# Output projection by token instance: 24 products per bank, and a last pass by token quarters

## The chip, the cores and the metric

The kernel runs on one core of a Trainium2 chip. The metric is device time in microseconds (us), the median of several executions. The core has five engines that run side by side and wait for each other through semaphores: TensorE (PE, with its weight loads shown as PEld), VectorE (DVE), ScalarE (ACT), GpSimd (POOL) and SyncE (SP). In this kernel nearly all transfers are issued by SP, in the order of its queue (SPq in the rows).

## The reference, cut to what matters

One decoder layer for a prompt of 1024 tokens and 8 sample tokens, 1032 tokens in all, with 1024 model columns. Everything is float32. The part that matters here:

```python
h = rmsnorm(x, w['norm1_w'])
proj = h @ w['w_in']
...                                   # HGRN2 heads -> o_a (1024 columns), Mamba-2 SSD -> y (1024 columns)
x = x + jnp.concatenate([o_a, y], axis=-1) @ w['w_out']
h = rmsnorm(x, w['norm2_w'])
gate, val = jnp.split(h @ w['w_up'], 2, axis=-1)
gate, buf_f_new = causal_dwconv(gate, buf_f, w['ffn_conv_w'], w['ffn_conv_b'])
x = x + (jax.nn.silu(gate) * val) @ w['w_down']
```

## The kernel before, in words

All activations lie transposed: 128 columns of the model per tile, tokens along the free axis. The 1032 tokens are four quarters of 258 (`QW`). Two quarters are an *instance* of the up projection (`hf` or `i` is 0 or 1). A float32 product is made of three matmuls on rounded halves (`steps`, `split`, `split_in`): weight high x activation high, high x low, low x high. So each weight block and each activation row is *split*: ACT casts the high half (`wh`, `mh`, `uh`), DVE subtracts to get the low half (`wl`, `ml`, `ul`). In this text a *product* is one such 128x128 by 258-column matmul on PE.

The order on PE is the order in which the code issues it (`manual_schedule`). Each PE step of the projections is one `tick`; `after(n, work)` issues work n ticks later, and `spread(pieces, n)` issues one piece every n ticks. The order on the other engines is made by the framework's planner from the dependences and the order of issue. `jobs` is the list of weight blocks in turn. When a job begins, the next one's weights are loaded (`load_ahead`, `wload`): one 512 KB DMA into `ws` (two buffers), the cast into `wh` and the subtraction into `wl` (two buffers each). `drive` mixes the steps of a stream, such as a `head`, between the products of the jobs up to a named one. `fetch` queues a load on SP behind the latest weight load.

The output projection has 16 row tiles: 0 to 7 from the HGRN heads, 8 to 15 from the SSD mixer. Each row tile lies in DRAM (`mix_d`); a head's tile is written at the end of that head (L1007). The jobs before:

- `o8.m` and `o12.m`: four row tiles, 256 output columns, all four token quarters, 96 products a job, a bank of 12 products each. The first sums are copied by ACT (L1076), the others added by DVE (L1078). The residual input is transposed on PE and added (`residual`). Head 7 runs beside the first of these jobs, up to `o12.2`.
- then for each instance `o0.m` and `o4.m`: four row tiles, 256 output columns, two quarters, 48 products a job. After the last four row tiles `final` stores the sum to `x1_d`, squares it on ACT and adds the square to `rst` on POOL.

So there are 24 weight blocks of 512 KB and 1536 products, and 128 banks are read out, 96 of them by DVE.

`set_norm` turns `rst` of one quarter into the second norm's factor. `set_of(i)` makes the seven operands p1 to p7 of the up projection from instance i (a seven-product scheme over two halves of the columns and two quarters of the tokens): `norm` scales the sums in place (L1171), `comb` makes sums and differences (L1189), `put` splits an operand (L1181, L1182). Before, `set_of` holds four temporaries of tag x5, which has five buffers, and the first up-projection weights (`up_load(0)`, two tiles of tag x5) are loaded inside `set_of(0)`, between `put` calls. POOL adds the weight sums (L1246) and `up_split` splits them (L1265, L1266). `set_of(0)` is issued beside the second instance's `o0` and `o4` jobs, `set_of(1)` 33 ticks into the first up step, whose products go first through instance 0, then through instance 1 (`ups(0, ...)`, 84 products each).

Of the kernel before, what the change touches and what calls it, by code (L numbers as in the profile page):

```python
# [1 line left out]

# [14 lines left out]
P = 128  # L17
DM = 1024
T = 1024
ND = 8  # L20
# [4 lines left out]
H = 8  # L25
# [25 lines left out]
def hybrid_layer(  # L51
# [219 lines left out]
    def drive(stream, weight, name):  # L271

        last = next(i for i, j in enumerate(jobs) if j[0] == name)
        left = sum(j[1] is not None for j in jobs[at[0]:last + 1]) * MMS
# [508 lines left out]
    def residual_load(m):  # L783
        ms = slice(m * P, (m + 1) * P)
        xs = [tl("d", "xs")[:, :512] for _ in range(2)]
        xd = small.tile([ND, P], F32, tag="xd", name=nm("xd"))
        for i in range(2):
            fetch(xs[i].rearrange("p (i m) -> p i m", m=P),
                  x_prompt[0, i * 512:(i + 1) * 512, ms].rearrange("(i p) m -> p i m", p=P))
        fetch(xd, x_sample[:, 0, ms])  # L790
        return xs, xd

    def residual(out, xs, xd):

        def add(x_, ps):
            V.tensor_tensor(x_, x_, ps, op=ALU.add)

        for i0 in range(2):
            ps = bank("xtp")
            for i in range(4):  # L800
                PE.transpose(ps[:, blk[i]], xs[i0][:, blk[i]], ident)
            if i0 == 0:
                add(out[0][:, 0:512], ps)
                ps = bank("xtd", "nx")
                PE.transpose(ps[:, :ND], xd, ident[:ND, :ND])
                add(out[1][:, 508:516], ps[:, :ND])
            else:
                add(out[0][:, 512:516], ps[:, 0:4])
                add(out[1][:, 0:508], ps[:, 4:512])
            yield  # L810
# [209 lines left out]
    def mix_load(r0):  # L1020

        lo = [tl("hT", "ml", F32R) for _ in range(4)]
        hi = [tl("hT", "mh", F32R) for _ in range(4)]
        for cs in chunks:
            for k in range(4):
                fetch(lo[k][:, cs].bitcast(F32), mix_d[r0 + k, :, cs])
        mixes[r0] = hi, lo

        def splits():
            for cs in chunks:  # L1030
                for k in range(4):
                    split_in(hi[k], lo[k], cs)
                    yield

        unsplit[r0] = splits()

    def split_rest(r0):
        for _ in unsplit[r0]:
            pass
# [455 lines left out]
```

## Time and profile before

| what | value |
|---|---|
| runs, us | 1795.12, 1800.53, 1799.58; median 1799.58 |
| the profiled execution's span, us | 1794.6 |
| PE busy | 1741.0 us, 97% |
| DVE busy | 1116.6 us, 62% |
| ACT busy | 789.1 us, 44% |
| POOL busy | 409.8 us, 23% |
| granted PE clock, mean | 0.992 |
| moved by DMA | 182.34 MB, mean 102 GB/s |

The span runs from the first to the last instruction of one profiled execution; the times of the runs hold what lies around it too. A busy time is the sum of the instructions' durations. Matmuls are pipelined and overlap in the record, so PE's speed is read from how far apart products start, or from how many of them a window holds. The output projection's products run from about 840 to 1065 us of the span, the first up step follows.

### The profile page before, as it was taken

How to read it: one execution, taken by the hardware profiler on the slowest of the kernel's cores; microseconds unless marked ns; L12 is line 12 of the kernel's file. 1: busy time of each engine (PE TensorE's matmuls, PEld its weight loads, DVE VectorE, ACT ScalarE, POOL GpSimd, SP SyncE). 2: the span in 40 equal slices, each digit the busy share in tenths (PEclk: the TensorE clock that was granted, in tenths of full speed). 3: DMA queues.
4: the chain of work that ended last, by engine and by line, in shares of the span. 5: the costliest groups of instructions: out<-in, count | busy, mean ns of one | idle time of the engine just before them, and what ended most of it. 6: DMA issues, size and time to landing. Idle time of an engine off the chain costs nothing.

```text
span 1794.6 us, 38584 instructions
## 1 busy us (share of the span) xinstructions
PE 1741.0 (97%) x16215; PEld 1685.0 (94%) x16215; DVE 1116.6 (62%) x2002; ACT 789.1 (44%) x1414; POOL 409.8 (23%) x415
## 2 busy tenths in 40 slices
PE   7999899999999999999999988999999999999998
PEld 7998798999999999999999978999999999999997
DVE  4658967556555564557746769666666667555545
ACT  6477688454544444345323344333433334111114
POOL 1103331110110110110100364455444542000001
PEclk9999999999999999999999998999999999999999
DMA  5135634553222221235334431222222225422212
GB/s 154 36 98 155 171 100 138 175 147 99 72 77 63 78 79 50 74 96 159 94 107 130 133 116 48 94 73 71 75 85 90 72 71 193 150 95 96 96 60 95
DMA packets 218018, 182.34 MB, mean 102 GB/s; under 512 B 13388, under 2 KB 195158, under 8 KB 217830
## 3 DMA queue, kind: packets, MB, share of 16 engines
q1 hardware_dynamic: 217558, 179.80, 32.5%
q8 instruction: 127, 2.08, 0.5%
q14 instruction: 45, 0.37, 0.1%
q0 software_dynamic: 288, 0.10, 0.0%
HBM read 141.53 MB, written 38.52 MB: 100 GB/s over the span
## 4 chain that ended last, share of the span: by engine, by line
PE 77%; DVE 8%; ACT 6%; DMA 5%; issue 2%; POOL 2%; SPq 0%; DVEq 0%; POOLq 0%; ACTq 0%
PE mm L93 30%; PE ub L93 14%; PE dn L93 13%; PE ua L93 10%; PE a L93 2%; PE o L93 1%; DMA csb<-cs_d 1%; ACT csb L549 1%; PE tp L93 1%; DVE wl L189 1%; DMA Bb<-bc_d 1%; PE kv L93 1%; DMA Sd<-in_state_ssm_dram 1%; DMA out_dram<-Sd 1%; DVE xbc L352 1%
## 5 line engine op out<-in xcount | busy, mean ns | idle before, releaser
L93 PE MATMUL mm<-hh,wh 128*128 128x344 f32 x1248 | 406.2, 326 | 2.6 <-ACT sz L685 2.6
L93 PE MATMUL mm<-hl,wh 128*128 128x344 f32 x1248 | 403.9, 324 | 0.0
L93 PE MATMUL mm<-hh,wl 128*128 128x344 f32 x1248 | 402.8, 323 | 0.0
L93 PEld LDWEIGHTS mm<-hh,wh 128*128 128x128 f32 x1248 | 234.6, 188 | 5.9 <-ACT sz L685 2.9
L93 PEld LDWEIGHTS mm<-hh,wl 128*128 128x128 f32 x1248 | 234.9, 188 | 2.4 <-issue 1.2
L93 PEld LDWEIGHTS mm<-hl,wh 128*128 128x128 f32 x1248 | 234.6, 188 | 2.5 <-issue 0.9
L188 ACT CAST wh<-ws 128x1024 fp32r<-128x1024 f32 x96 | 100.6, 1048 | 265.4 <-PE dn L93 135.8
L93 PE MATMUL ub<-ul,wh 128*128 128x258 f32 x704 | 199.6, 284 | 4.2 <-DVE ul L1182 4.2
L93 PE MATMUL ub<-uh,wh 128*128 128x258 f32 x704 | 201.1, 286 | 2.0 <-ACT uh L1181 2.0
L93 PE MATMUL ub<-uh,wl 128*128 128x258 f32 x704 | 200.8, 285 | 0.0
L93 PE MATMUL dn<-ah,wh 128*128 128x256 f32 (+1 forms) x640 | 180.7, 282 | 1.2 <-DVE x L1425 1.2
L93 PE MATMUL dn<-al,wh 128*128 128x256 f32 (+1 forms) x640 | 180.3, 282 | 0.0
L93 PE MATMUL dn<-ah,wl 128*128 128x256 f32 (+1 forms) x640 | 179.9, 281 | 0.0
L93 PE MATMUL mm<-mh,wh 128*128 128x258 f32 x512 | 148.2, 290 | 10.7 <-DVE x L1078 8.1
L189 DVE TENSOR_TENSOR wl<-ws,wh 128x1024 fp32r<-128x1024 f32 x96 | 125.3, 1306 | 52.5 <-ACT wh L188 52.3
L93 PE MATMUL ua<-ul,wh 128*128 128x258 f32 x528 | 148.9, 282 | 0.9 <-DVE ul L1182 0.9
L93 PE MATMUL ua<-uh,wl 128*128 128x258 f32 x528 | 149.4, 283 | 0.0
L93 PE MATMUL ua<-uh,wh 128*128 128x258 f32 x528 | 149.2, 282 | 0.0
L93 PE MATMUL mm<-ml,wh 128*128 128x258 f32 x512 | 146.5, 286 | 0.0
L93 PE MATMUL mm<-mh,wl 128*128 128x258 f32 x512 | 146.1, 285 | 0.0
L93 PEld LDWEIGHTS ub<-ul,wh 128*128 128x128 f32 x704 | 134.6, 191 | 4.9 <-DVE ul L1182 4.9
L93 PEld LDWEIGHTS ub<-uh,wh 128*128 128x128 f32 x704 | 134.2, 191 | 2.5 <-ACT uh L1181 2.5
(331 smaller groups left out, 3925.0 us busy)
## 6 DMA issues: line engine op xcount, KB each, us to landing
ws<-in_w_in_dram SPq DMA_DIRECT2D x52, 512.0 KB
ws<-in_w_up_dram SPq DMA_DIRECT2D x44, 512.0 KB
ws<-in_w_out_dram SPq DMA_DIRECT2D x24, 512.0 KB
act_d<-val SPq DMA_DIRECT2D x22, 516.0 KB
al<-act_d SPq DMA_DIRECT2D x22, 516.0 KB
ws<-in_w_down_dram SPq DMA_DIRECT2D x22, 512.0 KB
ml<-mix_d SPq DMA_DIRECT2D x48, 172.0 KB
csb<-cs_d SPq DMA_DIRECT2D x32, 256.0 KB
```

The source lines that it names most:

```text
L93: PE.matmul(out, lhsT, rhs, start=start, stop=stop)
L188: A.copy(wh[:, :n], ws[:, :n])
L189: V.tensor_tensor(wl[:, :n], ws[:, :n], wh[:, :n].bitcast(F32), op=ALU.subtract)
L352: V.scalar_tensor_tensor(acc[:, :n], ext[:, q:q + n], col(wname, q * ntile + j), acc[:, :n], op0=ALU.mult, op1=ALU.add)
L549: A.activation(csb3[:, h, :], csb3[:, h, :], AF.Relu, scale=-1.0, bias=cst[:, h0 + h:h0 + h + 1])
```

## The change

The jobs of the output projection are cut anew into four passes. Pass a takes row tiles 8 to 15 for instance 0, pass b row tiles 0 to 7 for instance 0, pass c row tiles 8 to 15 for instance 1, pass d row tiles 0 to 7 for instance 1. A job of a, b and c has eight row tiles, 128 output columns and two quarters: 48 products in two banks of 24. Pass d runs through all eight column tiles for its first quarter (`d00` to `d07`) and then, with the weights loaded again, for its second (`d10` to `d17`): 16 jobs of 24 products. There are 40 weight blocks of 512 KB in place of 24, and 64 banks read out in place of 128, 32 by ACT and 32 by DVE. The rows of the mix are loaded by instance, high and low half in one buffer. The residual is loaded and transposed once per instance, its adds come eight ticks after its transposes. Row 7, the last head's, is loaded when head 7 is done, and pass b begins two jobs later.

`set_of` uses two temporaries, one of its combinations moves from POOL to DVE, and operand p5 comes before p6. `set_of(0)` is issued through passes c and d, one piece every 14 ticks in place of 9. The first up weights are loaded 60 ticks into pass d and their first two splits issued at 120 and 150. For instance 1 the first quarter is normed, and p2 made, during the second half of pass d; the second quarter's norm follows 20 ticks into the first up step.

The diff, cut to its core:

```diff
-    def residual_load(m):
+    def residual_load(m, hf):
         ms = slice(m * P, (m + 1) * P)
...
+        xs = tl("t" if hf else "d", "xs")[:, :512]
...
+    def residual(out, hf, xs, xd):
...
+        n = ND if hf else 4
+        ps = bank("xtp")
+        for i in range(4):
+            PE.transpose(ps[:, blk[i]], xs[:, blk[i]], ident)
+        pd = bank("xtd", "nx")
+        PE.transpose(pd[:, :n], xd, ident[:n, :n])
+        yield
+        c = 4 * hf
+        add(out[:, 0:512 - c], ps[:, c:512])
+        add(out[:, 512 - c:], pd[:, :n])
...
-    def mix_load(r0):
...
+    MID = 2 * QW
+
+    def mix_rows(r0, hf):
...
+        for k in range(8):
+            t = tl("hT", "mx", F32R)
+            hi, lo = t[:, :MID], t[:, MID:]
+            fetch(lo.bitcast(F32), mix_d[r0 + k, :, hf * MID:(hf + 1) * MID])
+            mixes[key][0].append(hi)
+            mixes[key][1].append(lo)
+            todo.append((hi, lo))
+            yield
...
-    def out_job(r0, m, halves=(0, 1), last=False):
+    def out_job(name, r0, hf, m, cols=(0, 1), begin=None):
+        first, last = r0 == 8, r0 == 0
+
         def load():
-            w = wload(w_out[0, r0 * P:(r0 + 4) * P, m * P:(m + 2) * P], 4, 2 * P)
-            return w, [residual_load(m + i) for i in range(2)] if r0 == 8 else None
+            w = wload(w_out[0, r0 * P:(r0 + 8) * P, m * P:(m + 1) * P], 8)
+            return w, residual_load(m, hf) if first else None
...
+            for c in cols:
+                cs, ts_ = slice(c * QW, (c + 1) * QW), slice((2 * hf + c) * QW, (2 * hf + c + 1) * QW)
+                ps = psmm.tile([P, 512], F32, tag="mm", name=nm("mm"))[:, :QW]
+                yield from steps(w, 0, P, hi, lo, cs, ps)
+                x_ = xh[hf][m][:, cs]
+                if first:
+                    A.copy(x_, ps)
+                else:
+                    V.tensor_tensor(x_, x_, ps, op=ALU.add)
+                    final(m, x_, ts_)
+                yield True
+            if first:
+                spread(residual(xh[hf][m], hf, *res), 8)
...
-    for r0, ms in ((8, (0, 2)), (12, (0, 2)), (8, (4, 6)), (12, (4, 6))):
-        for m in ms:
-            out_job(r0, m)
-    for hf in range(2):
-        for r0 in (0, 4):
-            for m in range(0, KT, 2):
-                out_job(r0, m, (hf,), r0 == 4)
...
+    def open_b():
+        split_rest(0, 0)
+        mix_load(8, 1)
+        split_behind(60, 30, 8, 1)
+
+    def open_c():
+        split_rest(8, 1)
+        mix_load(0, 1)
+        split_behind(60, 30, 0, 1)
+
+    for m in range(KT):
+        out_job(f"a{m}", 8, 0, m, begin={0: open_a, 2: ahead_b}.get(m))
+    for m in range(KT):
+        out_job(f"b{m}", 0, 0, m, begin={0: open_b}.get(m))
+    for m in range(KT):
+        out_job(f"c{m}", 8, 1, m, begin={0: open_c}.get(m))
+    for c in range(2):
+        for m in range(KT):
+            out_job(f"d{c}{m}", 0, 1, m, (c,), {0: lambda: split_rest(0, 1)}.get(m + c))
...
-            drive(head(h, heads[h]), 32.0 if h else 35.0, f"sg{h + 1}" if h < H - 1 else "o12.2")
-        finish("o12.6")
-        mix_load(4)
-        after(24, lambda: spread(unsplit[4], 12))
...
+        drive(head(H - 1, heads[H - 1]), 32.0, "a5", 288)
+        for _ in rest_b[0]:
+            pass
+        after(10, lambda: spread(unsplit[0, 0], 8))
+        finish("a7")
...
-        def norm(h1):
+        def norm(h1, cols=slice(0, MID)):
...
+        if i == 0:
+            yield from norm(0)
+            yield from norm(1)
+            yield from put("p2", a2, "big")
+            yield from put("p4", b2, "e")
+        else:
+            yield from norm(1, c0)
+            yield from put("p2", a2, "big")
+            yield from norm(0, c0)
+            yield from put("p1", a1, "hT")
+            yield from norm(1, c1)
+            yield from put("p4", b2, "hT")
+            yield from norm(0, c1)
+        sa, sb = (quads(tl("x5", "sm")[:, :NT]) for _ in range(2))
+        yield from comb(sa, V, b1, b2, ALU.subtract)
+        yield from comb(sb, G, a1, b1, ALU.subtract)
         if i == 0:
-            while "o0.6.1" not in done:
+            while "c7" not in done:
                 yield
             yield from put("p1", a1, "hT")
...
+        yield from put("p5", [sa], "hT")
+        yield from comb(sa, V, two(sa), a1, ALU.subtract)
+        yield from put("p6", [sa], "hT")
+        yield from put("p7", [sb], "big" if i else "hT")
+        yield from comb(sa, V, two(sa), a2, ALU.add)
+        yield from put("p3", [sa], "big")
...
-    FIRST = ("p1", "p2", "p4", "p6", "p5", "p7", "p3")
+    FIRST = ("p1", "p2", "p4", "p5", "p6", "p7", "p3")
...
-        finish("o4.6.0")
+        finish("b7")
         after(16, lambda: set_norm(0, 0))
         after(30, lambda: set_norm(0, 1))
-        after(36, lambda: spread(set_of(0), 9))
-        finish("o4.6.1")
+        after(36, lambda: spread(set_of(0), 14))
+        finish("c7")
+        after(60, lambda: up_load(0))
+        after(120, lambda: up_split(0, 0))
+        after(150, lambda: up_split(0, 1))
+        finish("d07")
+        after(20, lambda: set_norm(1, 0))
+        second = set_of(1)
+        early = islice(second, 10)
+        after(40, lambda: spread(early, 8))
+        finish("d17")
         while len(usets[0]) < 7:
             tick()
         up_split(0, 2)
         up_split(0, 3)
-        after(20, lambda: set_norm(1, 0))
-        after(29, lambda: set_norm(1, 1))
-        after(33, lambda: spread(set_of(1), 2))
+        for _ in early:
+            pass
+        after(20, lambda: set_norm(1, 1))
+        after(24, lambda: spread(second, 2))
```

## Rows read from the trace of the kernel before

**Rows 1.** The page, part 1: busy us, share of the span, instructions.

```profile
PE 1741.0 (97%) x16215; PEld 1685.0 (94%) x16215; DVE 1116.6 (62%) x2002; ACT 789.1 (44%) x1414; POOL 409.8 (23%) x415
```

**Rows 2.** Windows: length, busy us (xinstructions) of PE PEld DVE ACT POOL, clock, DMA share, GB/s.

```profile
900.00:1000.00 100.00, 99.98 (x828) 99.02 (x827) 50.14 (x102) 32.27 (x61) 6.58 (x9) 1.00 0.42 129
...
1040.00:1065.00 25.00, 18.06 (x134) 17.36 (x133) 15.28 (x22) 8.90 (x19) 19.83 (x20) 0.86 0.45 126
...
1065.00:1110.00 45.00, 36.98 (x268) 35.07 (x268) 37.74 (x55) 19.78 (x33) 18.03 (x17) 0.89 0.11 32
...
1100.00:1120.00 20.00, 20.00 (x169) 20.00 (x168) 17.06 (x26) 10.10 (x16) 12.37 (x14) 1.00 0.27 85
```

**Rows 3.** Timeline of ACT and DVE, quiet jobs: start us, us, instruction, [idle before, releaser].

```profile
990.00 1.05 ACT L188 CAST wh<-ws 128x1024 fp32r<-128x1024 f32 x1 [0.49 <-PE mm L93]
...
995.75 1.05 ACT L188 CAST wh<-ws 128x1024 fp32r<-128x1024 f32 x1 [0.49 <-PE mm L93]
...
991.08 1.23 DVE L189 TENSOR_TENSOR wl<-ws,wh 128x1024 fp32r<-128x1024 f32 x1 [0.58 <-ACT wh L188]
```

**Rows 4.** Timeline of PE at 1053 us.

```profile
1053.31 0.58 PE L93 MATMUL mm<-mh,wh 128*128 128x258 f32 x1 [6.75 <-DVE x L1078]
...
1053.91 0.42 PE L93 MATMUL mm<-mh,wl 128*128 128x258 f32 x1
1054.12 0.42 PE L93 MATMUL mm<-mh,wh 128*128 128x258 f32 x1
```

**Rows 5.** Timeline of ACT and DVE, 1046 to 1051 us.

```profile
1046.95 0.62 ACT L1265 CAST wh<-wt 128x512 fp32r<-128x512 f32 x1 [5.49 <-POOL wt L1246]
...
1050.04 1.74 DVE L1266 TENSOR_TENSOR wl<-wt,wh 128x512 fp32r<-128x512 f32 x2 [5.29 <-ACT wh L1265]
```

**Rows 6.** Timeline: PE's first up-projection product, and DVE at 1090 us.

```profile
1065.08 0.28 PE L93 MATMUL ua<-uh,wh 128*128 128x258 f32 x1
...
1090.22 5.19 DVE L1182 TENSOR_TENSOR ul<-sm,uh 128x1032 fp32r<-128x1032 f32 x4
```

**Rows 7.** Groups by line and shape, 880 to 1110 us: xcount | busy us, mean ns | idle.

```profile
L1078 DVE TENSOR_TENSOR x<-x,mm 128x258 f32<-128x258 f32 x96 | 39.5, 417 | 33.9 <-PE mm L93 33.9
...
L1182 DVE TENSOR_TENSOR ul<-x,uh 128x516 fp32r<-128x516 f32 x12 | 9.6, 803 | 0.0
...
L1182 DVE TENSOR_TENSOR ul<-sm,uh 128x1032 fp32r<-128x1032 f32 x8 | 10.2, 1301 | 0.0
...
L1266 DVE TENSOR_TENSOR wl<-wt,wh 128x512 fp32r<-128x512 f32 x8 | 8.3, 1064 | 5.5 <-ACT wh L1265 5.5
...
L1171 DVE SCALAR_TENSOR_TENSOR x<-x,vcol,n2r 128x516 f32<-128x516 f32 x16 | 13.7, 885 | 0.1
```

**Rows 8.** Timeline of SP's queue and of the first reader, two loads.

```profile
1723.11 5.98 SPq L1435 DMA_DIRECT2D ws<-in_w_down_dram  x2
...
1726.42 1.05 ACT L1011 CAST wdh<-ws 128x1024 fp32r<-128x1024 f32 x1 [4.59 <-DMA ws<-in_w_down_dram]
...
1122.49 0.37 SPq L1238 DMA_DIRECT2D ws<-in_w_up_dram  x1
...
1126.42 1.28 POOL L1246 TENSOR_TENSOR wt<-ws 128x512 f32<-128x512 f32 x1 [8.21 <-DMA ws<-in_w_up_dram]
```

**Rows 9.** Instructions by tile ws: duration ns min/median/max, first and last start.

```profile
L189 DVE TENSOR_TENSOR wl<-ws,wh x96: 1203/1225/2330, 10.9 to 1734.5; 128x1024 fp32r<-128x1024 f32 x96
```

**Rows 10.** Timeline of ACT and SP's queue at the end of head 7.

```profile
893.25 1.26 ACT L659 ACTIVATE sq<-hms,epsc 128x512 f32<-128x512 f32 x2 [1.80 <-issue]
...
900.09 0.34 SPq L1007 DMA_DIRECT2D mix_d<-sg  x1
```

**Rows 11.** Timeline of PE at 840 us, and the window after it.

```profile
840.00 0.38 PE L93 MATMUL mm<-mh,wh 128*128 128x258 f32 x1 [2.50 <-ACT sg L826]
...
840.00:845.00 5.00, 5.00 (x50) 4.67 (x54) 5.00 (x9) 3.72 (x9) 0.94 (x1) 0.66 0.59 193
```

**Rows 12.** Instructions by tile xtd: duration ns min/median/max.

```profile
L805 PE MATMUL xtd<-ident,xd x8: 223/223/223, 850.6 to 937.0; 8*128 8x8 f32 x8
```

More of the change, by code (lines that the diff above doesn't have):

```diff
@@ L1 @@
 from contextlib import ExitStack
+from itertools import islice
 import concourse.bass as bass
@@ L269, in finish, with drive @@
             step(name)
-    def drive(stream, weight, name):
-        last = next(i for i, j in enumerate(jobs) if j[0] == name)
-        left = sum(j[1] is not None for j in jobs[at[0]:last + 1]) * MMS
+    def drive(stream, weight, name, left=None):
+        if left is None:
+            last = next(i for i, j in enumerate(jobs) if j[0] == name)
+            left = sum(j[1] is not None for j in jobs[at[0]:last + 1]) * MMS
         debt = 0.0
@@ L1084, in out_job @@
-        job(f"o{r0}.{m}" + (f".{halves[0]}" if len(halves) == 1 else ""), load, run)
+            if begin is not None:
+                begin()
+            hi, lo = mixes[r0, hf]
+            if first:
+                if m % 2 == 0:
+                    xpair[hf][m // 2] = tl("big", "x1")[:, :NT].rearrange("p (i t) -> p i t", i=2)
+                xh[hf][m] = xpair[hf][m // 2][:, m % 2, :]
+            for c in cols:
[9 more added lines that the diff above has]
+                yield True
@@ L1086, in final @@
+            if first:
+                spread(residual(xh[hf][m], hf, *res), 8)
+        job(name, load, run)
     def final(m, x_, ts_):
@@ L1112, in hybrid_layer, with split_behind, open_a, ahead_b @@
         heads[h] = head_in(h)
-    for r0, ms in ((8, (0, 2)), (12, (0, 2)), (8, (4, 6)), (12, (4, 6))):
-        for m in ms:
-            out_job(r0, m)
-    for hf in range(2):
-        for r0 in (0, 4):
-            for m in range(0, KT, 2):
-                out_job(r0, m, (hf,), r0 == 4)
+    def split_behind(n0, n, *key):
+        after(n0, lambda: spread(unsplit[key], n))
+    def open_a():
+        mix_load(8, 0)
+        split_rest(8, 0)
+    def ahead_b():
+        heads_rows = mix_rows(0, 0)
+        def load():
+            for k in range(7):
+                next(heads_rows)
+        load()
+        rest_b.append(heads_rows)
+    rest_b = []
+    def open_b():
[15 more added lines that the diff above has]
+            out_job(f"d{c}{m}", 0, 1, m, (c,), {0: lambda: split_rest(0, 1)}.get(m + c))
     with tc.manual_schedule(engines={mybir.EngineType.PE}):
@@ L1126, in hybrid_layer @@
         finish("z7")
[L1127 to L1131 removed]
+        for h in range(H - 1):
+            drive(head(h, heads[h]), 32.0 if h else 35.0, f"sg{h + 1}")
+        drive(head(H - 1, heads[H - 1]), 32.0, "a5", 288)
[3 more added lines that the diff above has]
+        finish("a7")
     part.close()
```

116 lines of the change are left out of this document (24 added, 92 removed).

## The prediction

> **What bounds the kernel now.** I read the page first, then the busy time of each engine in windows, then the order of instructions inside the windows where TensorE (PE) falls short. PE is busy for 97% of the span [rows 1], so time can be won only where PE waits, or lost by making it wait. In the stretch 900 to 1000 us, inside the output projection, PE is busy 99.98 of 100 us [rows 2]: nothing done to VectorE (DVE), ScalarE (ACT) or the DMAs there can bring anything. The hole is where the output projection hands over to the up projection, 1040 to 1110 us. I price it by counting products. A 258-column product costs 0.118 us (169 in 20 us [rows 2]); quiet 48-product jobs follow each other every 5.75 us (their weight casts start at 990.00 and 995.75 [rows 3]), so 0.120 each there. Between 1040 and 1065 PE got through 134, worth 16.1 us: 8.9 us lost. Between 1065 and 1110 it got through 268, worth 31.7 us: 13.3 us lost [rows 2].
>
> The first hole is one wait of 6.75 us for a bank, and products 0.21 us apart after it, the lower clock level [rows 4]. The bank is emptied by DVE, but DVE itself waited 5.29 us for an ACT cast, and ACT waited 5.49 us for GpSimd's (POOL's) sums of the first up-projection weights [rows 5]. By the code those weights share the five slots of tag x5 with four temporaries of `set_of(0)`, so the second of them is loaded only when a temporary is free. The second hole: the operands of the second token instance are made after its last product, on DVE, which finishes the last one at 1090.22 + 5.19 = 1095.4, 30.3 us after the output projection ended at 1065.1 [rows 6].
>
> **The change part by part.** The products stay 1536, each of the same shape.
>
> *Banks of 24 products.* 64 evictions fewer on DVE, 64 x 0.42 = 26.9 us of DVE [rows 7]. They lie where PE never waits, so I cost them at nothing. The same for one instance at a time in passes a, b and c: weights come at 512 KB per 48 products, as in the jobs o0 and o4 of before, which hold the quiet cadence [rows 3].
>
> *Shorter x5 list, weights loaded ahead.* `set_of` now needs two temporaries, so two for it and two weight tiles fit in five slots, and the load stands 60 ticks before its first split. The 8.9 us should go. What is late next in that place is pass d.
>
> *Pass d by quarters.* It has 16 jobs of 24 products, 2.88 us each at 0.120, with 16 more weight loads, casts and subtractions than before. Each of the two staging buffers must be loaded, cast and subtracted within two jobs. From issue to cast a 512 KB load took 3.31 us (1723.11 to 1726.42), and 3.93 us to its POOL reader (1122.49 to 1126.42) [rows 8]; from the cast's start to the subtraction's end is 1.08 + 1.23 = 2.31 us [rows 3]. One turn is thus 5.6 to 6.2 us, against 5.75 available: 0 to 0.25 us lost per job. I take 0.15, nearer the second load because its short runs are those of the new weight blocks: 2.4 us over 16 jobs. In the first eight jobs (23.0 us) DVE also has the tail of `set_of(0)`: 8 subtractions at 1.23 (the median [rows 9]) and 8 adds at 0.42 are 13.2 us, two half puts at 0.80, four whole puts at 1.30 and four combination pieces (no row here; priced as a half put, 0.80) are 10.0 us, four weight halves near 1.0 are 4.0 us [rows 7]. Together 27.2 us, 4.2 more than the eight jobs have. In the second eight DVE has 13.2 + 8 half-width norms at 0.44 + two puts at 0.80 + three small steps at 0.42, 19.6 us of 23.0, so it can catch up part. A job's subtraction queued behind a put delays PE; I take the 4.2 us plus 1.0 for gaps in which DVE waits for ACT. Pass d: 7.6 us. Its low end is 0 (DVE's overflow moves into the second half and loads take 3.31 us). Its high end: every turn takes 3.93 + 1.08 + 2.33 (the longest subtraction seen, same row) + 0.1 = 7.4 us, so 3.7 per job, 16 x 0.84 = 13.4 us.
>
> *Second instance's operands.* The first quarter's norm and p2 are made during the second half of pass d; p1 needs no further norm. After the last product DVE still has three weight halves (3.0), five bank reads of the first instance (2.1), a norm (1.3), eight half-width norms (3.5), p1 and p4 (3.2), six combination pieces (4.8) and four whole puts (5.2): 23.1 us in place of the 30.3 us seen. PE reaches p3 of the second instance after 156 products and two norm sums, about 19.2 us. So 3.9 us stay, plus 1.0 us for the two norm sums on PE themselves (no row; each taken as four products), which the 13.3 held too: 4.9 us remain. The bounds are 1 us (PE waits nowhere, since p1, p2 and p4 come in the order in which they are ready) and 9 us (the same lateness, and the clock falls as in the first hole).
>
> *Head 7 to pass b.* Pass b needs row 7, the last head's. From the head's last root on ACT to the issue of its store 6.84 us passed [rows 10]; store 3.93, reload 3.31 (by [rows 8]; the store's 516 KB is about that size, the reload's 258 KB half of it), split 0.6 on ACT and 0.8 on DVE: 15.5 us. Head 7's steps weigh 28.2 of 32, so they end 254 products into the 288; 34 + 96 + 21 products, 18.1 us, lie between that and the first product with row 7. I cost it at nothing; if the cover is gone, up to 4 us. SP stands still while it waits for the store; behind it are weight loads that have two jobs of 5.75 us.
>
> *Start of pass a.* PE needs eight rows of one instance in place of four of both; it waits 2.50 us there already for banks of the projection [rows 11]. The bytes are equal and the splits are half: 0, between -2 and +2.
>
> *Residual.* Eight more small transposes at 0.22 us or less [rows 12]: 1.0 us. The token norm, the x1 stores and the POOL adds are the same in number.
>
> Sum: -22.2 + 7.6 + 4.9 + 1.0 = -8.7 us against a span of 1794.6: 1785.9. The runs' median 1799.58 stands 5.0 us above that profiled span; with the same 5.0, **1791 us**, 0.5% faster.
>
> **Rivals.**
> *A. Pass d runs freely.* DVE's overflow slips and loads land early: d costs 1, the seam 3, the transposes 1: 1799.6 - 22.2 + 5 = 1782.4. For it: the jobs of before kept their cadence with the same casts and subtractions [rows 3]. Against: there a job had 5.75 us for them, not 2.88.
> *B. Pass d is bound by its weights.* 13.4 us there and 7 at the seam: 1799.6 - 22.2 + 13.4 + 7 + 1 = 1798.8. No change that can be measured. For it: the turn of 5.6 to 6.2 us against 5.75; the store of x1 shares the DMA engines.
> *C. The clock falls in pass d: slower.* After the 2.50 us wait at 837.5 the granted clock of 840 to 845 was 0.66 [rows 11], so a single wait of this size can end in the lower level of 1.2 GHz, where a product takes 0.215 us [rows 4]. A job of 24 then takes 5.2 us in place of 2.88 and hides its own supply. Twelve of 16 such jobs cost 12 x 2.3 = 28 us in place of the 7.6: 1811. It decides from the point at which pass d has waits as long as that one; the estimate of 0.5 us per job speaks against it. The Trainium skill (TensorE: Matmul & The Clock Gate, "HAM oscillation — how this bites in real kernels") says that batches of matmuls shorter than the wait for their next operand keep a kernel at the low clock; by that rule all 16 jobs would be at the low level, and the time 1820. The trace of before agrees for its two long waits; no row here shows many short ones.
> *D. The change does not do what it says: the early pieces do not run early.* If DVE is behind by the second half of d, p2 and the norms still fall behind the last product and the seam keeps 13: 1799.
> *E. Row 7 is late at pass b.* 4 us and some clock: 1797.
>
> **How the numbers follow.** Forecast 0.43 (own range 1786 to 1797), A 0.15, B 0.20, C 0.11, D 0.06, E 0.05. The range that leaves no more than 2 in 10 out: 1783 to 1804. A measurement of this kernel can tell 0.3%, 5.4 us, from no change: faster is below 1794.2, slower above 1805.0. Faster: 0.33 of the forecast's 0.43, A's 0.15, 0.03 of B, total 0.51. Slower: C's 0.10, 0.04 of B and 0.01 of D, total 0.15. The rest, 0.34, is the same.
>
> **What would show it.** In the profile after: PE's wait of 6.75 us and the ACT wait on POOL are gone; no wait at the first bank of pass b longer than 2 us; in the first half of pass d PE waits for `wl` (DVE) or `wh` (ACT) of some 0.5 to 1 us at job starts, sum 5 to 10 us, clock at 1.00; the products of the second instance in the first up step wait 2 to 6 us in all. If pass d's casts wait for their DMA, B holds; if the granted clock there is under 0.9, C. If waits appear before pass d, in a, b or c, this reading of the covers was wrong.

## The result, and the profile after

The changed kernel took 1807.1 us (median of 22 runs, 1799.64 to 1815.6) beside 1799.89 us for the kernel before (1794.15 to 1807.02): a ratio of 1.0036, 95% interval 1.0024 to 1.0048. Measured a second time it took 1805.46 us, a ratio of 1.0024 (1.0009 to 1.0040). It is slower by 5 to 7 us where 8.7 us of gain were forecast, and lies above the forecast range.

Two profiles of it were taken. The first is of the longest of its 22 executions (1815.6 us, span 1813.9), the second of an execution of 1806.89 us (span 1805.2), the longest but one of the eight of the second measurement and close to the first median. Readings are from the first unless the second is named; sizes are taken from the second where they differ.

PE's share of the span is what it was [rows 1], its busy time is not:

```profile
PE 1751.8 (97%) x16223; PEld 1693.6 (93%) x16223; DVE 1116.1 (62%) x1950; ACT 802.6 (44%) x1414; POOL 409.9 (23%) x411
```

The waits of PE from 836 to 1120 us, first profile (engine, tile and line, what it waited for: us in total, times, longest):

```profile
PE a L94 <- DVE q L878: 6.3, 2, 5.4
PE mm L94 <- DVE wl L190: 4.3, 8, 1.1
PE n2ms L94 <- DVE nt L662: 3.4, 1, 3.4
PE n2ms L94 <- POOL n2r L1096: 3.2, 1, 3.2
PE ub L94 <- ACT uh L1214: 2.2, 1, 2.2
...
PE ub L94 <- DVE ul L1215: 1.5, 1, 1.5
PE mm L94 <- ACT wh L189: 1.5, 2, 0.9
```

The wait of 6.75 us [rows 4] is gone. In its place stand four others: head 7's attention in pass a (`a<-q,k`), the norm sums of the first instance at the start of pass c (`n2ms <- nt`), the weights in pass d (`wl`, `wh`), and the seam to the up projection (`n2ms <- POOL`, then `uh`, `ul`). Busy time and clock around them (windows; columns as in [rows 2]):

```profile
860.00:880.00 20.00, 13.64 (x297) 12.44 (x295) 12.92 (x23) 8.02 (x17) 0.00 (x0) 0.83 0.70 213
970.00:990.00 20.00, 16.59 (x110) 15.66 (x108) 15.31 (x24) 9.04 (x17) 5.58 (x5) 0.83 0.69 206
1032.00:1085.00 53.00, 47.20 (x371) 45.05 (x371) 38.58 (x55) 26.95 (x40) 17.15 (x13) 1.00 0.65 183
1085.00:1120.00 35.00, 28.14 (x186) 27.04 (x185) 24.35 (x43) 12.36 (x21) 12.44 (x11) 0.80 0.05 16
```

In the kernel before, PE was busy for 99.98 of 100 us in the middle of the output projection [rows 2]. Now two stretches there fall to a mean clock of 0.83, on top of the waits. Pass d (the third line) keeps 1.00 in this profile and is short of work only: 371 products are worth 43.8 of its 53 us.

**Head 7.** Timeline of SP's queue, ACT, DVE and PE, in the order of cause:

```profile
855.67 4.68 SPq L861 DMA_DIRECT2D out_dram<-Sh  x2
...
862.01 4.21 SPq L179 DMA_DIRECT2D mx<-mix_d  x7
...
866.46 0.62 ACT L1018 CAST mx<-mx 128x516 fp32r<-128x516 f32 x1 [10.98 <-DMA mx<-mix_d]
...
867.12 2.28 DVE L1019 TENSOR_TENSOR mx<-mx 128x516 fp32r<-128x516 f32 x3 [5.67 <-ACT mx L1018]
...
870.75 1.09 PE L94 MATMUL a<-q,k 128*32 128x32 f32 x64 [5.39 <-DVE q L878]
```

The rows of pass b are loaded behind a head's state store, which SP issues up to 860.35; their loads are issued from 862.01. The casts and subtractions of these rows stand in ACT's and DVE's queues ahead of head 7's own steps. So ACT stands for 10.98 us and DVE for 5.67 us over rows that nobody needs before pass b, whose first product starts at 923.54, and head 7's `q`, which is needed now, stands behind them.

**Start of pass c.** The same pattern, with the rows of pass d ahead of the first instance's norm (timeline of ACT, DVE, PE):

```profile
974.75 1.31 ACT L1018 CAST mx<-mx 128x516 fp32r<-128x516 f32 x2 [3.48 <-DMA mx<-mix_d]
...
975.40 1.38 DVE L1019 TENSOR_TENSOR mx<-mx 128x516 fp32r<-128x516 f32 x2 [3.20 <-ACT mx L1018]
976.71 0.42 DVE L662 SCALAR_TENSOR_TENSOR nt<-n2ms,n2r 128x258 f32<-128x258 f32 x1
...
977.27 1.20 PE L94 MATMUL n2ms<-n2r,ones 128*128 128x258 f32 x2 [3.41 <-DVE nt L662]
```

**Pass d.** Its first and last bank reads, 15 jobs apart (DVE), and what its weight casts wait for (waits, 1030 to 1092 us):

```profile
1033.13 0.42 DVE L1081 TENSOR_TENSOR x<-x,mm 128x258 f32<-128x258 f32 x1
...
1085.01 0.41 DVE L1081 TENSOR_TENSOR x<-x,mm 128x258 f32<-128x258 f32 x1
```

```profile
ACT wh L189 <- DMA ws<-in_w_out_dram: 16.2, 11, 2.7
```

(1085.01 - 1033.13) / 15 = 3.46 us a job in place of 2.88.

**The seam.** Timeline of POOL, PE and DVE:

```profile
1087.03 1.26 POOL L1274 TENSOR_TENSOR wt<-ws 128x512 f32<-128x512 f32 x1 [3.71 <-DMA ws<-in_w_up_dram]
...
1089.59 0.64 POOL L1096 TENSOR_TENSOR n2r<-n2r,n2sq 128x258 f32<-128x258 f32 x1
...
1090.29 1.23 PE L94 MATMUL n2ms<-n2r,ones 128*128 128x258 f32 x2 [3.19 <-POOL n2r L1096]
...
1092.06 0.43 DVE L662 SCALAR_TENSOR_TENSOR nt<-n2ms,n2r 128x258 f32<-128x258 f32 x1 [6.03 <-ACT n2r L661]
```

POOL makes the weight sums of the *second* up step, whose load it waits for, ahead of the last square that PE waits for now. The same weights would have been needed 168 products later.

To compare kernels I read three marks from PE's timeline: the last product of the input projection, the last of the output projection, and the 168th of the up projection (its first step). "Projection" is the time from the first to the second mark, "seam" the time from the first up product to the 168th less 168 x 0.118 = 19.8 us [rows 2], "job" the spacing of pass d's bank reads. What follows the last mark takes 696 to 698 us in every kernel. The three marks of the kernel before, then those of the second profile:

```profile
837.07 0.32 PE L93 MATMUL mm<-hh,wl 128*128 128x344 f32 x1
...
1064.95 0.28 PE L93 MATMUL mm<-mh,wl 128*128 128x258 f32 x1
...
1098.65 0.28 PE L93 MATMUL ua<-uh,wl 128*128 128x258 f32 x1
...
840.45 0.32 PE L94 MATMUL mm<-hh,wl 128*128 128x344 f32 x1
...
1077.77 0.28 PE L94 MATMUL mm<-mx,wl 128*128 128x258 f32 x1
...
1108.78 0.28 PE L94 MATMUL ua<-uh,wl 128*128 128x258 f32 x1
```

| kernel | projection, us | job, us | seam lost, us |
|---|---|---|---|
| before | 227.9 | | 13.8 |
| changed, first profile | 241.7 | 3.46 | 13.4 |
| changed, second profile | 237.3 | 3.50 | 11.1 |
| e1: pass b's rows behind head 7 | 232.2 | 3.46 | 10.8 |
| e2: pass d's rows behind the norm | 235.6 | 3.51 | 10.9 |
| e3: third staging buffer | 230.0 | 3.11 | 11.9 |
| e4: POOL's sums behind the square | 237.5 | 3.42 | 10.1 |
| g3: e1 and e2 | 230.7 | 3.44 | 11.8 |
| f1: e1, e2 and e4 | 228.4 | 3.46 | 9.8 |
| f2: f1 and e3 | 222.7 | 3.11 | 9.5 |
| f3: f1, pass d whole | 220.4 | 2.85 | 15.4 |
| f4: f2 without the last norm | 227.6 | 3.19 | 5.2 |
| g2: f2, tiles 0 to 3 of pass d whole | 220.8 | 3.03 | 13.1 |

### The profile page after: what moved, and what is told of

The parts are those of the page before. It is cut to its first block, busy times and chain, and to the rows that moved or that the text cites. A ratio compares the mean times of both kernels' runs of the same rounds, so it can differ in the third digit from the quotient of the medians.

```text
span 1813.9 us, 38558 instructions
## 1 busy us (share of the span) xinstructions
PE 1751.8 (97%) x16223; PEld 1693.6 (93%) x16223; DVE 1116.1 (62%) x1950; ACT 802.6 (44%) x1414; POOL 409.9 (23%) x411
## 4 chain that ended last, share of the span: by engine, by line
PE 44%; DVE 2%; DMA 2%; ACT 1%; issue 1%; POOL 0%; DVEq 0%; ACTq 0%; POOLq 0%
PE ub L94 14%; PE dn L94 13%; PE ua L94 10%; PE mm L94 6%; DMA ws<-in_w_out_dram 1%; DVE wl L190 1%; DVE ul L1215 0%; DMA mx<-mix_d 0%; DVE x L1204 0%; DMA ws<-in_w_up_dram 0%; PE xtp L805 0%; PE fin L1488 0%; DVE sm L1220 0%; ACT wh L189 0%; ACT ot L1490 0%
## 5 line engine op out<-in xcount | busy, mean ns | idle before, releaser
L94 PEld LDWEIGHTS mm<-hl,wh 128*128 128x128 f32 x1248 | 235.7, 189 | 2.5 <-issue 0.9
L189 ACT CAST wh<-ws 128x1024 fp32r<-128x1024 f32 x112 | 117.7, 1050 | 268.8 <-PE dn L94 134.2
L190 DVE TENSOR_TENSOR wl<-ws,wh 128x1024 fp32r<-128x1024 f32 x112 | 146.9, 1312 | 92.3 <-ACT wh L189 92.1
L94 PE MATMUL mm<-mx,wh 128*128 128x258 f32 x1024 | 193.3, 289 | 3.6 <-ACT sg L827 1.6
L94 PEld LDWEIGHTS mm<-mx,wh 128*128 128x128 f32 x1024 | 160.7, 191 | 5.4 <-ACT sg L827 2.0
L94 PE MATMUL mm<-mx,wl 128*128 128x258 f32 x512 | 147.2, 288 | 4.3 <-DVE wl L190 4.3
```

Source lines behind the costliest of these rows:

```text
L94: PE.matmul(out, lhsT, rhs, start=start, stop=stop)
L189: A.copy(wh[:, :n], ws[:, :n])
L190: V.tensor_tensor(wl[:, :n], ws[:, :n], wh[:, :n].bitcast(F32), op=ALU.subtract)
```

## The experiments

**Theory.** Four separate causes: row splits queued ahead of head 7, row splits queued ahead of a norm, weight blocks of pass d through two staging buffers, and POOL's sums ahead of the last square. **Rivals:** the waits are chance of one execution; or ACT and DVE are simply full, and a wait taken away in one place returns in the next.

### One cause at a time

`e1_rows_behind_head` gives the splits of pass b's rows a place in the queues of ACT and DVE: behind the last root of head 7 (`rstd_of` now returns its ACT and DVE instructions, `queued(key)` puts what it holds behind those in `behind[key]`).

```diff
             for hi, lo in todo:
-                split_in(hi, lo, slice(0, MID))
+                with queued(key):
+                    split_in(hi, lo, slice(0, MID))
                 yield
...
-            rstd_of(sq[hf], half("nt"), ps, P)
+            behind[0, 0] = rstd_of(sq[hf], half("nt"), ps, P)
```

> The splits of pass b's mix rows (ACT casts, DVE subtractions) are queued behind head 7's last root and correction; nothing else changes. Theory Q (work that waits for a DMA stands ahead of head 7's steps in the in-order queues of ACT and DVE): the waits of PE in head 7 for DVE (6.3 us in the changed kernel's profile, the longest 5.4) fall under 1 us, the granted clock of 860 to 880 is back at 1.00, and the time falls by 5 to 9 us. Theory W (only pass d's weight supply took the gain): the time moves by less than 2 us.

Measured: 1799.08 us, ratio to before 0.9994 (0.9983 to 1.0006). That is 6.4 to 8.0 us under the two medians of the changed kernel, as the theory had it. Head 7's waits shrink to 1.6 us in sum, the longest 0.9 where under 1 was expected, the clock of 860 to 880 is back at 1.00, and the wait at the start of pass c shrinks as well:

```profile
PE n2ms L94 <- DVE nt L669: 1.9, 1, 1.9
PE a L94 <- DVE q L885: 1.6, 2, 0.9
```

With this one place in two queues mended the change is neutral.

`e2_rows_behind_norm` does the same for pass d's rows, behind `set_norm(0, 1)`; the splits are queued as in e1.

```diff
-        rstd_of(rst[:, cs], tl("us", "nt"), ps[:, :QW], DM)
+        r = rstd_of(rst[:, cs], tl("us", "nt"), ps[:, :QW], DM)
+        if (i, c) == (0, 1):
+            behind[0, 1] = r
```

> The splits of pass d's mix rows are queued behind the correction of the second quarter's norm factor; nothing else changes. Theory Q: PE's wait of 3.4 us before the second norm sum at the start of pass c goes, and the lower clock behind it; the time falls by 3 to 5 us. Theory W: less than 2 us.

Measured: 1802.67 us, 1.0022 (1.0009 to 1.0035), 4.4 us under the first median of the changed kernel and 2.8 under the second, where 3 to 5 were expected. The wait at the start of pass c is gone, that for head 7 stands:

```profile
PE a L94 <- DVE q L885: 6.2, 3, 4.3
```

`e3_third_staging`: every third weight block of pass d goes into a buffer of its own.

```diff
+        turn[0] += third
+        if third and turn[0] % 3 == 0:
+            ws = tmp.tile([P, KT * P], F32, tag="ws3", bufs=1, name=nm("ws"))
```

> Every third weight block of pass d is staged in a third buffer, so a load can be issued one job earlier; nothing else changes. Theory W (a staging buffer's turn of load, cast and subtraction takes longer than two jobs): ACT's waits for the weight loads in pass d fall from 16.2 us in 11 casts to under 5, the 16 jobs take 46 to 50 us in place of about 58, and the time falls by 7 to 10 us. Rival (DVE is over-full in pass d, as the prediction had it): the jobs still take over 54 us, waiting for DVE and ACT, and the time falls by less than 3 us.

Measured: 1801.45 us, 1.0009 (0.9997 to 1.0022). The gain of 4.0 to 5.7 us misses the 7 to 10 that were expected; the two signs in pass d came. The casts' wait for loads falls from 16.2 us in 11 to 0.9 us in one; they now wait for PE to give their `wh` buffers back (waits, 1010 to 1062 us):

```profile
ACT wh L195 <- PE mm L94: 13.9, 9, 2.4
```

A job takes 3.11 us: of the 0.6 us that each job lost, the staging buffers were some 0.35.

`e4_sums_behind_square`: the second up step's weight sums behind the last add to `rst`.

```diff
-            G.tensor_tensor(rst[:, ts_], rst[:, ts_], sq, op=ALU.add)
+            behind["pool"] = [G.tensor_tensor(rst[:, ts_], rst[:, ts_], sq, op=ALU.add)]
...
+            with queued("pool" if j == 1 else None):
+                G.tensor_tensor(sums[name], x_, y_, op=ALU.add)
```

> POOL's sums of the second up step's weights are queued behind the last add of squares; nothing else changes. Theory Q: PE's wait of 3.2 us for the last norm sum and DVE's idle 6.0 us before it go, the waits for the second instance's operands shrink, and the time falls by 3 to 6 us. Rival (the second instance's operands are bound by DVE's work anyway): the wait moves to the operands and the time falls by less than 2 us.

Measured: 1802.99 us, 1.0016 (1.0003 to 1.0029), 4.1 or 2.5 us under the two medians: theory (3 to 6) by the one, between theory and rival (under 2) by the other. The wait for POOL is gone, and DVE's idle time before the last norm falls from 6.03 (4.51 in the second profile) to 2.06 us. Part of it comes back a few products later, two waits each for `uh` and `ul` in place of one:

```profile
PE ub L94 <- DVE ul L1222: 2.8, 2, 1.4
PE ub L94 <- ACT uh L1221: 2.4, 2, 1.4
```

The seam loses 10.1 us where the two profiles of the changed kernel show 13.4 and 11.1.

### Is it chance? The changed kernel once more

> The changed kernel as it stands, for a second profile of it: the first profiled execution was the longest of its 22 (1815.6 us), and between the last product of head 7's gate input and the 168th product of the up projection it took 275.05 us, 13.5 more than the kernel before, where the medians differ by 7.2. Theory (the four waits are in every execution, and only their size and the stretches at the lower clock behind them vary): the time is 1807 us, 1804 to 1810; the waits for head 7 in pass a stand at 4 to 6 us in sum, pass d at 3.45 us a job, a wait for POOL of 2 to 4 us at the seam; the stretch takes 266 to 271 us. Rival (the waits of the first profile were chance of that execution): no wait of over 2 us for head 7 or for the norm, and the stretch within 3 us of before's 261.6.

No edit. Measured: 1805.46 us, 1.0024 (1.0009 to 1.0040). Waits of PE, second profile:

```profile
PE a L94 <- DVE q L878: 6.9, 4, 3.3
PE mm L94 <- DVE wl L190: 3.5, 5, 1.1
PE ub L94 <- ACT uh L1214: 2.2, 1, 2.2
PE n2ms L94 <- POOL n2r L1096: 2.2, 1, 2.2
PE mm L94 <- ACT wh L189: 1.8, 2, 1.0
PE ub L94 <- DVE ul L1215: 1.4, 1, 1.4
PE n2ms L94 <- DVE nt L662: 1.3, 1, 1.3
```

The same waits in the same places; from the first mark to the last 268.3 us against 261.6 before, 6.7 us more, within the 4.9 to 7.2 of the medians. Not chance. The waits for head 7 are 6.9 us in sum where 4 to 6 were expected. Only the norm's wait at pass c was larger in the first profile than it usually is (3.4 against 1.3 here).

### Do the causes add up?

> The two reorderings of the row splits (pass b's behind head 7, pass d's behind pass c's norm) without that of POOL's weight sums: taken alone they gave 8.0 and 4.4 us, all three together 10.8 and not 16.5. Theory (the first two overlap: one split that is moved also lets the other wait shrink, as the norm wait fell from 3.4 to 1.9 us with the first alone): the two together give 8 to 9 us, 1798 to 1799 us, and POOL's sums another 2 to 3 on top. Rival (the third overlaps with the first two, since the seam's last wait only changes its place): the two together give what the three give, 1795.5 to 1797 us.

Measured: 1797.67 us, 0.9985 (0.9975 to 0.9995). It falls between the two expectations, and its interval (1796.0 to 1799.6 us) reaches into both: what overlaps with what is not settled. Its profiled execution (span 1802.1) was not one of its short ones.

> The three reorderings together: pass b's row splits behind head 7's last root, pass d's row splits behind pass c's norm, POOL's weight sums of the second instance behind the last residual square. Theory (three separate waits, each the fault of a place in an in-order queue, that add up): the single gains against the changed kernel's 1807.1 us were 8.0, 4.4 and 4.1, so 1790.6 us, 1788 to 1794, a ratio of 0.993 to 0.997 to the kernel before; PE's waits for head 7 under 2 us in sum, no wait over 2 us for the norm at the start of pass c, pass d still at about 3.45 us a job. Rival (ACT and DVE are full over the whole stretch from pass a to pass d, so a wait that is removed in one place comes back in the next): the sum does not add, 1796 to 1800 us, and new PE waits of 4 us or more in passes b to d.

Measured: 1796.3 us, 0.9977 (0.9964 to 0.9990). The three single gains, taken against the two medians of the changed kernel, sum to 16.6 or 11.6 us; together they give 10.8 or 9.2. The sum I expected, 1790.6, was too good, in part because it rested on the first median: by the second it would have been 1793.8, still 2.5 us too good. The rival's time fits, but not its mechanism: no wait over 1.5 us is left on PE before the last mark, and none of 4 us has come back in passes b to d; only the waits for `uh` and `ul` at the seam have grown, from 3.6 to 4.8 us. What is left is pass d at 3.46 us a job, and the clock: waits of 1.01 and 0.76 us, which end at 1030.52 and 1031.78, stand at the head of ten microseconds at 0.83.

```profile
1030.00:1040.00 10.00, 8.69 (x55) 8.29 (x56) 4.77 (x6) 4.19 (x7) 2.13 (x2) 0.83 0.51 151
```

> The three reorderings and, on top, a third staging buffer for pass d's weight blocks. Theory (pass d is held by the supply of weights through two staging buffers, and that is independent of the queue places): alone the third buffer gave 5.6 us, so 1785 us, 1783 to 1789, a ratio of 0.990 to 0.994; pass d at 3.1 us a job, no ACT cast of pass d's weights that waits for a load. Rival (in pass d the casts of ACT and the splits of DVE are the bound as soon as the loads are not, and the row work that now lies later falls into it): 1790 us or above, the same as the three reorderings alone, pass d at 3.3 us a job or more with PE waiting for the casts.

Measured: 1789.61 us, 0.9944 (0.9928 to 0.9961): 10.4 us faster than the kernel before and 15.9 to 17.5 faster than the changed one. Against f1 it gains 6.7 us, a little more than the third buffer alone. The level expected, 1785, was again 4 to 5 us too good, for the same reason: from the second median the four gains sum to 1789.8. Pass d stands at (1060.79 - 1014.16) / 15 = 3.11 us a job, as foreseen:

```profile
1014.16 0.41 DVE L1095 TENSOR_TENSOR x<-x,mm 128x258 f32<-128x258 f32 x1
...
1060.79 0.41 DVE L1095 TENSOR_TENSOR x<-x,mm 128x258 f32<-128x258 f32 x1
```

### What are the quarters worth?

`f3_queues_whole_pass_d` is f1 without pass d's split by quarters, and so without the norm and the operand pieces that ran early under it:

```diff
-    for c in range(2):
-        for m in range(KT):
-            out_job(f"d{c}{m}", 0, 1, m, (c,), {0: lambda: split_rest(0, 1)}.get(m + c))
+    for m in range(KT):
+        out_job(f"d{m}", 0, 1, m, begin={0: lambda: split_rest(0, 1)}.get(m))
...
-        after(20, lambda: set_norm(1, 0))
         second = set_of(1)
-        early = islice(second, 10)
-        after(40, lambda: spread(early, 8))
...
-        after(20, lambda: set_norm(1, 1))
+        after(20, lambda: set_norm(1, 0))
+        after(29, lambda: set_norm(1, 1))
```

> The three reorderings, with pass d undone to whole jobs: eight jobs of 48 products (all four row tiles) in place of sixteen of 24 by quarters, so each weight block is loaded and cast once, and no row work of the second instance starts before the pass ends. Theory (the quarters cost 9 us in pass d by loading and casting the weights twice and give back only part of the seam, which went from 13.8 us over the ideal to 10 to 13): pass d loses 0 to 2 us, the seam loses 13 to 17, in sum 1789 to 1795 us, the same as the reorderings with the quarters within 4 us. Rival (the quarters are worth what they were made for; without them the seam takes the whole chain of both quarters, 20 us or more): 1798 to 1803 us.

Measured: 1792.92 us, 0.9969 (0.9950 to 0.9987), as the theory had it. No cast in pass d waits for a load, and 24 products take (1060.06 - 1017.31) / 15 = 2.85 us. The seam pays for it, 15.4 us:

```profile
1017.31 0.41 DVE L1089 TENSOR_TENSOR x<-x,mm 128x258 f32<-128x258 f32 x1
...
1060.06 0.42 DVE L1089 TENSOR_TENSOR x<-x,mm 128x258 f32<-128x258 f32 x1 [2.47 <-PE mm L94]
...
1082.32 0.58 PE L94 MATMUL ub<-uh,wh 128*128 128x258 f32 x1 [4.63 <-ACT uh L1223]
```

So with two staging buffers the quarters give 15.4 - 9.8 = 5.6 us at the seam and take 16 x (3.46 - 2.85) = 9.8 us in pass d; in the medians f3 stands 3.4 us below f1, with intervals that overlap. With three buffers they take 16 x 0.26 = 4.2 and give 5.9: a gain of 1.7 by these two terms, of 3.5 by the whole stretch between the marks (252.1 us in f2, 255.7 in f3), and of 3.3 in the medians, again with intervals that overlap.

`g2_last_four_tiles_by_quarter` is f2 with only the last four column tiles by quarters; since the cover is half as long, its early pieces also follow each other every 5 ticks in place of 8:

```diff
+    for m in range(4):
+        out_job(f"d{m}", 0, 1, m, begin={0: lambda: split_rest(0, 1)}.get(m))
     for c in range(2):
-        for m in range(KT):
-            out_job(f"d{c}{m}", 0, 1, m, (c,), {0: lambda: split_rest(0, 1)}.get(m + c))
+        for m in range(4, KT):
+            out_job(f"d{c}{m}", 0, 1, m, (c,))
...
-        after(40, lambda: spread(early, 8))
+        after(40, lambda: spread(early, 5))
```

> The three reorderings and the third buffer, with pass d by quarters only in its second half: output tiles 0 to 3 whole (48 products to a weight block), tiles 4 to 7 by quarters (24 to a block). Theory (the quarter split costs pass d by the blocks that are fetched and cast twice, in proportion to their number, 0.25 us a job with the third buffer, and the first quarter's norm and splits need only some 10 us of cover, which eight short jobs give): pass d gives back 2 us, the seam loses the same 9 to 10 us over the products as with all tiles by quarters, so 1787 to 1789 us, at most 2 us under the 1789.6 of the kernel with all tiles by quarters. Rival (the early pieces need the whole first half of pass d as cover): the seam loses 12 us or more and the time is 1791 us or above.

Measured: 1794.43 us, 0.9961 (0.9945 to 0.9976): my expectation was wrong and the rival holds. Pass d gives back 1.2 us (15 x 0.08), the seam loses 3.6 more. With less cover the first quarter's norms and splits still run when the pass ends, and the second quarter's norm comes behind them on DVE, 6.0 us after the last bank read (3.0 with f2). Timeline of DVE; the last bank read is the second row:

```profile
1062.00 1.66 DVE L1222 SCALAR_TENSOR_TENSOR x<-x,vcol,n2r 128x258 f32<-128x258 f32 x3
1063.58 0.41 DVE L1095 TENSOR_TENSOR x<-x,mm 128x258 f32<-128x258 f32 x1
...
1066.17 3.48 DVE L1233 TENSOR_TENSOR ul<-x,uh 128x516 fp32r<-128x516 f32 x2
1069.58 0.41 DVE L675 SCALAR_TENSOR_TENSOR nt<-n2ms,n2r 128x258 f32<-128x258 f32 x1
```

### What is the seam made of?

`f4_no_second_norm` is f2 without the norm of the last quarter, whose rows are scaled with the first quarter's factor:

```diff
-            rs = rst[:, ts_][:, cols]
+            rs = rst[:, ts_][:, slice(0, QW) if i and cols.start else cols]
...
-        after(20, lambda: set_norm(1, 1))
```

> As the kernel with the reorderings and the third buffer, but the norm of the last quarter (second instance) is left out and its rows are scaled with the first quarter's factor: this leaves out part of the computation, the last square sums, their adds on POOL, the norm sum on PE and the root, and the last quarter's output is not the reference's. It prices the chain at the seam. Theory (the seam is a chain of latencies: last square, POOL add, norm sum, root, scaling): without it the seam loses 5 us or less over the products' own time, and the time falls by 5 to 8 us against the kernel with the norm. Rival (the seam is work: DVE and ACT have so much of the last rows' scaling and splitting to do that the chain is hidden behind it): the seam still loses 8 us or more, and the time falls by less than 3 us.

Measured: 1788.16 us, 0.9940 (0.9921 to 0.9960). The expectation counts the last squares and their adds on POOL among what is left out; the edit leaves them in (the last add runs at 1067.32) and takes out the norm sum, the root and the correction, and with them the wait for the adds. The seam falls from 9.5 to 5.2 us, so that chain is worth 4.3 us there; one wait of 3.2 us is left, for a bank that DVE reads late (`fext`). The time does not show the 4.3: it falls by 1.5 us, within the intervals, where the theory had 5 to 8. In the profiled execution the projection took 4.9 us more than in f2, with an idle of 1.68 us of PE's own in pass a, for which the profile names no releaser, the window 870 to 880 at 0.83, and 3.19 us a job in pass d. By the seam the theory is nearly met (5 us or less), by the time the rival's sign came (less than 3 us): what the chain is worth in kernel time stays open.

## Why the prediction was wrong, step by step

The second profile gives the sizes. A run whose passes have next to no such losses stands in for the ideal: f3, with its projection of 220.4 us, of which 218.5 from its first product.

| step of the sum | forecast, us | measured, us | how |
|---|---|---|---|
| first hole, with the residual transposes | -7.9 | -6.5 | 218.5 (f3) - 225.0 (before), first to last product of the projection |
| pass d | +7.6 | +9.7 | 15 x (3.50 - 2.85) |
| head 7, and start of pass c | 0 | +7.5 | 235.7 - 218.5 - 9.7 |
| seam | -8.4 | -2.7 | 11.1 - 13.8 |
| start of pass a | 0 | -1.3 | 1.6 (second profile) - 2.9 (before), last input product to first product of pass a |
| sum | -8.7 | +6.7 | |

The third row is a remainder. Counted directly, from the first product of each pass to the first of the next, it comes out nearly the same: against f3, pass a of the second profile is 6.25 us longer (79.10 and 72.85), pass b equal (46.24), pass c 1.50 longer (54.79 and 53.29) and pass d, from its first to its last product, 9.48 (55.58 and 46.10). In the first profile they are 5.9, 0, 6.4 and 8.9. With e1, pass a takes 73.1 us.

**The first hole** went, as read from [rows 4, 5]. The 6.5 us are what f3 keeps of it, with the new transposes and small waits of f3's own in pass a (0.89 and 0.75 us); they do not show that the 8.9 us of loss were read wrongly.

**Pass d** was mis-sized by 2 us, within its bounds. The kind of wait was as foreseen, 0.2 to 1.1 us at job starts, 5.8 in sum, and rival B's sign came, casts that wait for their DMA. The terms were not: what I took as 0.15 us per job from the weights (2.4 us) was some 0.35 by e3 (5.6 us), and DVE's over-full first half, priced at 5.2 us, does not show. The first half is no slower than the second (3.43 and 3.49 us a job in the first profile), and with the third buffer (f2) it stands at 3.02, 8 x 0.17 = 1.4 us over f3. That the sum was only 2 us off is in part luck.

**"Head 7 to pass b ... I cost it at nothing"** is the first step that failed. I asked when row 7 would be ready and who was queued behind SP's wait, and priced the weight loads there. I did not ask about the *other seven rows* of pass b, whose loads stand in the same place of SP's queue and whose splits stand in the queues of ACT and DVE. The casts that waited for these loads held up on ACT, and through it on DVE, everything that stood behind them, though the first of them ran 57 us before pass b began (866.46 and 923.54 in the first profile). Row 7 itself came in time: no wait stands at the start of pass b, so the nothing was right for the one row that I looked at. The trace of before could not show the rest; the order of issue in the changed code could have raised it: `ahead_b` loads the rows while head 7 is running. The last sentence of the prediction had named this test, and it failed it. e1 shows that the place in the queue is the cause: 8.0 us against the first median, 6.4 against the second.

**The start of pass c** is the same fault in small, and was not priced at all. e2 removes the wait.

**The seam** is the second step that failed: 4.9 us were to remain, with 9 as the upper bound; 13.4 and 11.1 remain in the two profiles. I had added up DVE's work, 23.1 us, as a block without gaps. In the trace DVE stands idle for 6.03 us in the middle of it (4.51 in the second profile), since its next step needs the chain square, POOL, norm sum, root. The chain was left out of the sum, though the trace of before has it: DVE stood idle for 3.19 us there ahead of the same step (the first line below, from the trace of before; the others are of the second profile). Without the last norm the seam loses 5.2 us (f4), close to the 4.9 forecast, but that is another kernel, and its time did not show the gain. The second thing left out is that a wait costs more than its length. The waits at the seam of the second profile sum to 2.16 + 2.18 + 1.40 = 5.7 us, of which 11.1 are lost, with the clock at 0.83 from 1080 to 1090 and at 0.66 from 1100 to 1110. In the kernel before, 8.0 us of waits cost 13.8. The clock is not all of it: norm sums on PE lie within these losses too, and a wait costs more than its length even at full clock. In pass d of the first profile, with the clock at 1.00, ten waits of 5.8 us in sum go with a loss of 9.2 (53 us less 371 x 0.118): the profile counts a wait from the end of the product before it, 0.28 us after its start, where the next would have started after 0.118, and the second product behind a wait comes some 0.22 us after the first.

```profile
1069.87 0.43 DVE L660 SCALAR_TENSOR_TENSOR nt<-n2ms,n2r 128x258 f32<-128x258 f32 x1 [3.19 <-ACT n2r L659]
...
1080.00:1090.00 10.00, 7.84 (x51) 7.58 (x50) 5.40 (x12) 2.00 (x4) 4.93 (x5) 0.83 0.00 1
...
1100.00:1110.00 10.00, 7.90 (x46) 7.61 (x47) 8.71 (x14) 4.77 (x8) 0.62 (x1) 0.66 0.00 0
```

**The rivals.** B had the right mark in pass d, and with 9.7 in place of its 13.4 us. C did not come: the clock of pass d stood at 1.00 through ten waits of up to 1.1 us in the first profile, and fell in two windows of the second only (0.96 and 0.87, 1050 to 1070 us); e2, e4 and f1 have ten microseconds at 0.83 there each. The rule of the Trainium skill (TensorE: Matmul & The Clock Gate, "HAM oscillation — how this bites in real kernels") is about batches shorter than the wait for their next operand; a job of 24 products with a wait of up to 1.1 us is not one, so rival C had applied it where it does not reach, and these traces do not speak against it. Head 7 agrees with it: some 4 us of work from 861.24 stand ahead of the wait of 5.39, and 870 to 880 stood at 0.80. The falls at the seam, around waits of 2.2 to 3.2 us behind much longer work, are not of its kind. D did not come in its own terms, since the early pieces did run early (the norm of the first quarter from 1060.53 in the first profile, 24 us before the last bank read), but the 13 us that it left at the seam were nearly met, since what came after them was held up by POOL. E looked at row 7 alone. No rival held a wait in pass a.

**The offset.** I added 5.0 us to the forecast span because the median stood that far above it. That is no part of the miss: -8.7 us were forecast against +7.2 and +4.9 in the medians and +6.7 in the table, and the offset enters none of these differences.

What stays open: how much of the loss that overlaps between e1, e2 and e4 belongs to which, and what the chain at the seam is worth in kernel time. The 0.26 us a job that pass d still loses with three buffers is not spread over the jobs: f2 has three waits of PE there, 1.10 and 0.17 us for `wl` and 0.63 for the first quarter's norm sum, at a clock of 1.00.

## What to carry to other kernels

When a change loads something earlier, or spreads its preparation through other work, write down for every engine which instruction of it waits for the load, and what stands behind that instruction in the queue; here early loads became free of cost only when the work that waits for them was queued late. Price a hand-over by its longest chain of dependent steps as well as by the sum of the busiest engine's work, and take a wait of PE at more than its length: here at 1.6 times at full clock, and at up to twice where the clock fell. A split into smaller jobs that fetches the same weights twice needs its staging checked first: here the split lost 3.4 us with two buffers and gained 3.3 with three, by medians whose intervals overlap.

## What the runs showed of the hardware

The granted clock can fall after waits of about 1 us: in pass d it stood at 0.83 in the ten microseconds with, or just behind, a pair of waits of 1.01 and 0.76 us (f1), 1.15 and 0.75 (e2) and 1.07 and 0.76 (e4), and from 870 to 880 in f4 after its idle of 1.68 us. Yet a wait of 1.10 us (f2, at 1020.76), a pair of 0.87 and 0.75 in pass d of the changed kernel's first profile, and a pair of 1.09 and 1.39 at f2's seam (1070 to 1080) left it at 1.00. The length of the waits alone does not tell whether it falls.

The subtraction of a weight block on DVE (128x1024) took at most 1.23 us in the 83 cases of the first profile with less than 0.2 us of POOL's work beside it, and up to 2.33 us in the other 29.
